# Two of a transformer layer's matrix products by Strassen's scheme, with sums of weights made in DRAM

## The chip, the cores and the metric

The kernel runs on one core of one Trainium2 chip. A core has engines that each work through a queue of their own: TensorE (PE, matrix products into PSUM), VectorE (DVE) and ScalarE (ACT, elementwise work), GpSimd (POOL, elementwise work and some DMAs), and SyncE (SP, here the queue that issues most DMAs). They meet by semaphores: an instruction that has to wait holds up all that stand behind it on its engine. The metric is device time in microseconds for one execution, and lower is better.

## The reference

One layer with sliding-window attention over 512 positions, width 2048, and a gated per-layer embedding. All is float32.

```python
hn = rmsnorm(x, norm_g)
q, k, v, gate = split(hn @ w_in)                     # 2048, 256, 256, 2048 columns
# 32 heads of 64 in 4 groups, blocks of 128 positions, window 128:
scores = q @ k.T * 64 ** -0.5 + rel_bias[bucket]     # own block and the one before
probs  = softmax of scores with one sink per head    # causal, inside the window
y = (probs @ v * silu(gate)) @ w_out                 # 512 x 2048 by 2048 x 2048
x = x + y
emb = p @ ple_proj                                   # 512 x 256 by 256 x 2048
g = sigmoid(rmsnorm(x, ple_norm) @ ple_gate)         # 512 x 2048 by 2048 x 2048
x = x + emb * g
out = rmsnorm(x, final_g)
```

The change is in the two products with w_out and ple_gate, and in how the loads are ordered.

## The kernel before

Matrix products keep float32 accuracy in three passes: an operand is split into hi (rounded to the fast format `fp32r`) and lo (the rest), and `mm3` (L113 to 117) issues hi x hi, lo x hi and hi x lo. So each product of 128 x 128 by 128 x 512 is three matmuls.

The weights come in pieces of 128 x 1024 float32 (512 KB). The class `Weights` makes each: SP loads it into `wraw` (L85), ACT casts it to `whi` (L86), DVE subtracts to get `wlo` (L87). Each of the three names has three buffers, and pieces are made two ahead of their use.

The stages follow one another on PE:

1. The start (L160 to 205): 16 steps over the 128-row blocks of x transposed, which make the first columns of q, all of k and v, in eight PSUM banks. Then the evacuation: q is split (`qe`, `qo`, L214 to 217), the scale per position `rb` is read out, k and v are scaled, split and stored as `K`, `V` and `DV` (L232 to 273), with small subtractions on POOL (L235).
2. The projections of the other q and gate columns (L426 on), 30 groups of 16 steps of three matmuls. They are interleaved with the 64 blocks of attention: `steps` (L456) places the scores of block i, the transposition of its probabilities and their product with v between steps of the projections. Each pair of heads needs a bias tile, which SP loads from a small table in DRAM (`load_bias`, L283). When four gate columns are there, ACT applies silu to the group (L391) and POOL multiplies the four attention outputs in (`gate_value`, L388). `split_a` (L396) splits the result for the next product.
3. y: for each of the four blocks of 512 columns, 16 steps over k, each for four row blocks (L517). A piece of w_out feeds 24 matmuls. DVE adds the result to x (L529), ACT takes the squares for the norm, and x is transposed for the next stage between the steps (`turn_x`, L497).
4. g: the same with ple_gate, with the embeddings' products between. `finish` (L552 to 565) applies the sigmoid (ACT), the product with the embedding, the addition to x (DVE), the squares, and the product with final_g (POOL, L560). The last block of columns is done by row blocks (L583 on), so that the final norm and the stores of one row block run beside the next.

The order on PE is as written in the program. On the other engines, SP among them, a scheduler sets the order in the build.

Of the kernel before, what the change touches and what calls it, by code (L numbers as in the profile page):

```python
# [1 line left out]

# [15 lines left out]
D = 2048  # L18
# [15 lines left out]
WARM = 34  # L34

# [12 lines left out]
def trunk_kernel(ctx: ExitStack, tc: tile.TileContext, a: dict):  # L48
# [4 lines left out]

    const = pool("const")
    psum = pool("psum", bufs=2, space=PSUM)

    const.tile([P, 56], F32, name="pad")
    pn = const.tile([P, KC], F32, name="pn")
    acts = pool("acts", bufs=KC)
    wpool = pool("wpool", bufs=3)  # L60

# [6 lines left out]
    class Weights:  # L68


        def __init__(self, ahead):
            self.srcs, self.ahead, self.made, self.apart = [], ahead, [], set()

        def add(self, src, shape):
            self.srcs.append((src, shape))
            return len(self.srcs) - 1

        def _make(self, i):
            src, shape = self.srcs[i]
            if i in self.apart:  # L80
                return self._make_apart(i)
            raw = wpool.tile([P, WE], F32, tag="wraw", name=f"wraw{i}")
            hi = wpool.tile([P, WE], F32R, tag="whi", name=f"whi{i}")
            lo = wpool.tile([P, WE], F32R, tag="wlo", name=f"wlo{i}")
            nc.sync.dma_start(raw if len(src.shape) == 2 else raw.rearrange("p (k c) -> p k c", k=shape), src)  # L85
            nc.scalar.copy(hi, raw)  # L86
            nc.vector.tensor_sub(lo, raw, hi.bitcast(F32))  # L87
            v = lambda t: t.rearrange("p (k c) -> p k c", k=shape)
            self.made.append((v(hi), v(lo)))

        def _make_apart(self, i):

            raw = wpool.tile([P, WE], F32, tag="wraw", name=f"wraw{i}")
            nc.sync.dma_start(raw, self.srcs[i][0])
            his, los = [], []
            for k in range(2):
                r = raw[:, k * 512 : (k + 1) * 512]
                h = acts.tile([P, S], F32R, tag="ah", name=f"wh{i}_{k}")
                l = acts.tile([P, S], F32R, tag="al", name=f"wl{i}_{k}")
                nc.scalar.copy(h, r)  # L100
                nc.vector.tensor_sub(l, r, h.bitcast(F32))
                his.append(h)
                los.append(l)
            self.made.append((his, los))
# [35 lines left out]
    rb = const.tile([P, S], F32, name="rb")  # L140
# [16 lines left out]
    mid = ExitStack()  # L157
    kvq = mid.enter_context(tc.tile_pool(name="kvq", bufs=1))
    pre = ExitStack()
    start_pool = pre.enter_context(tc.tile_pool(name="start", bufs=3))  # L160

    for k in range(KC):
        xg = start_pool.tile([P, S + 1], F32, tag="xr", name=f"xr{k}")
# [6 lines left out]
        h = acts.tile([P, S], F32R, tag="ah", name=f"xh{k}")  # L170
        l = acts.tile([P, S], F32R, tag="al", name=f"xl{k}")
# [4 lines left out]
        wh = start_pool.tile([P, 768], F32R, tag="w0h", name=f"w0h{k}")  # L176
        wl = start_pool.tile([P, 768], F32R, tag="w0l", name=f"w0l{k}")
# [15 lines left out]
        if 3 <= k < 3 + NB:  # L193
            t = k - 3
            xn = start_pool.tile([P, D], F32, tag="xn", name=f"xn{t}", bufs=2)
# [5 lines left out]
        if k == 12:  # L201
            rcol = start_pool.tile([P, NB, P], F32, name="rcol", bufs=1)
            nc.vector.tensor_copy(rcol, rstd1.unsqueeze(2).to_broadcast([P, NB, P]))
# [22 lines left out]
    def evac_v():  # L226
        heads = lambda v: v.rearrange("p (h d) -> p h d", h=KVH)
        whole = []
        for t in range(NB):
            src = heads(v_ps[t][:, :256])  # L230
            whole.append(start_pool.tile([P, KVH * HD], F32, name=f"whole{t}", bufs=1))
            nc.vector.tensor_scalar_mul(heads(whole[t]), src, rstd1[:, t : t + 1])  # L232
        for t in range(1, NB):
            diff = start_pool.tile([P, KVH * HD], F32, name=f"diff{t}", bufs=1)
            nc.gpsimd.tensor_sub(diff, whole[t], whole[t - 1])  # L235
            for dst, v in ((V[t - 1], whole[t - 1]), (DV[t], diff)):
# [4 lines left out]
    relb = start_pool.tile([HEADS, BUCKETS], F32, name="relb", bufs=1)  # L241
    nc.gpsimd.dma_start(relb, a["rel"])
    tvec = start_pool.tile([HEADS, TOEP], F32, name="tvec", bufs=1)
# [17 lines left out]
    for t in range(2):  # L261
        kt = start_pool.tile([P, S], F32, tag="kt", name=f"kt{t}", bufs=1)
# [134 lines left out]
    def split_a(c):  # L397
        src = gates[c // 4][:, c % 4, :]
        ah[c] = acts.tile([P, S], F32R, tag="ah", name=f"ah{c}")
        al[c] = acts.tile([P, S], F32R, tag="al", name=f"al{c}")  # L400
        nc.scalar.copy(ah[c], src)
        nc.vector.tensor_sub(al[c], src, ah[c].bitcast(F32))

# [10 lines left out]
    for kind, c in kinds:  # L414
        for n in range(2):
            W.add(a["w_gate_in" if kind == "g" else "w_q"][c][:, n * WE : (n + 1) * WE], 8)
    for j in range(4):
        for n in range(8):
            W.add(a["w_out"][j, n], 2)
    for j in range(4):  # L420
        proj_w = a["ple_proj"].rearrange("(k p) d -> p k d", p=P)[:, :, j * 512 : (j + 1) * 512]
        if j == 3:
            W.add(proj_w, 2)
        for n in range(8):
            W.add(a["ple_gate"][j, n], 2)
        if j < 3:  # L426
            W.add(proj_w, 2)
    W.apart = set(range(len(W.srcs) - 8, len(W.srcs) - 2))

    def projections():  # L430
        for m, (kind, c) in enumerate(kinds):
            ps = bank(f"{kind}ps{c}", "p")
            for k in range(KC):
                wh, wl = W.get(2 * m + k // 8)
                mm3(ps, wh[:, k % 8, :], wl[:, k % 8, :], xh[k], xl[k], k == 0, k == KC - 1)
                if k == KC - 1:
                    if kind == "q":
                        evac_q(c, ps)
                    else:
                        g = c // 4  # L440
                        if c % 4 == 0:
                            gates[g] = apool.tile([P, 4, S], F32, name=f"gate{g}")
# [3 lines left out]
                if m == len(kinds) - 1 and k < 12:  # L446
                    split_a(k)
# [19 lines left out]
    for i in range(blocks):  # L467
# [3 lines left out]
        steps(i, todo)  # L471
    steps(blocks, 7)
    steps(blocks + 1, 7)
# [4 lines left out]
    for c in range(12, PAIRS):  # L478
        split_a(c)
    mid.close()  # L480


    late = pool("late", reuse_waits="tile")
    nc.gpsimd.dma_start(pn, a["ple_norm"])
    fg = late.tile([P, D], F32, name="fg")
    nc.gpsimd.dma_start(fg, a["final_g"].partition_broadcast(P))
    pTh = late.tile([P, 2, S], F32R, name="pTh")
    pTl = late.tile([P, 2, S], F32R, name="pTl")

    ssq2 = const.tile([P, NB, 4], F32, name="ssq2")  # L490
    ssq3 = const.tile([P, NB, 5], F32, name="ssq3")
    x1, hh, hl = [], {}, {}
    for j in range(4):
        x1.append(late.tile([P, NB, 512], F32, name=f"x1_{j}"))
        nc.sync.dma_start(x1[j], a["x"].rearrange("(t p) d -> p t d", p=P)[:, :, j * 512 : (j + 1) * 512])

    HALVES = ("sstt", "ppoo")  # L497

    def turn_x(k):

        j, kk = divmod(k, 4)
        tp = bank(f"tp{k}", HALVES[j % 2][kk])
        for t in range(NB):
            nc.tensor.transpose(tp[:, t * P : (t + 1) * P], x1[j][:, t, kk * P : (kk + 1) * P], ident)
        pl_, th, tl = (late, f"hh{k}", f"hl{k}") if j < 3 else (acts, "ah", "al")
        hh[k] = pl_.tile([P, S], F32R, tag=th, name=f"hh{k}")
        hl[k] = pl_.tile([P, S], F32R, tag=tl, name=f"hl{k}")
        nc.scalar.mul(hh[k], tp, pn[:, k : k + 1])
        nc.vector.scalar_tensor_tensor(
            out=hl[k], in0=tp, scalar=pn[:, k : k + 1], in1=hh[k].bitcast(F32), op0=ALU.mult, op1=ALU.subtract  # L510
        )

    def blk(t):
        return slice(t * P, (t + 1) * P)

    wi = 2 * len(kinds)
    turning = []  # L517
    for j in range(4):
        acc = [bank(f"y{j}_{t}", HALVES[j % 2][t]) for t in range(NB)]
        for k in range(KC):  # L520
            wh, wl = W.get(wi + k // 2)
            for t in range(NB):
# [131 lines left out]
```

## Time and profile before

| what | value |
|---|---|
| median of 3 runs | 865.29 us (864.97 to 866.22) |
| the profiled execution | 863.4 us, span 861.7 us |
| mean granted TensorE clock | 0.998 |
| busy: PE / DVE / ACT / POOL | 849.0 / 494.1 / 368.3 / 108.4 us |
| the start | 0 to 76 us |
| projections and attention | 76 to 474 us |
| y (w_out) | 474 to about 656 us |
| g (ple_gate and embeddings) | about 656 to 853 us |
| after the last matmul | 853 to 862 us |

Times in rows of the profile are microseconds from the start of the span unless marked ns. A row of a group gives the line, the engine, the operation with its tiles (out<-in), the shapes, the count, then the busy time and the mean duration in ns, then the idle time before it and what ended it. A row of a timeline begins with its start and its duration. Matmuls are pipelined, so their durations overlap.

### The profile page before, as it was taken

How to read it: one execution, taken by the hardware profiler on the slowest of the kernel's cores; microseconds unless marked ns; L12 is line 12 of the kernel's file. 1: busy time of each engine (PE TensorE's matmuls, PEld its weight loads, DVE VectorE, ACT ScalarE, POOL GpSimd, SP SyncE). 2: the span in 40 equal slices, each digit the busy share in tenths (PEclk: the TensorE clock that was granted, in tenths of full speed). 3: DMA queues.
4: the chain of work that ended last, by engine and by line, in shares of the span. 5: the costliest groups of instructions: out<-in, count | busy, mean ns of one | idle time of the engine just before them, and what ended most of it. 6: DMA issues, size and time to landing. Idle time of an engine off the chain costs nothing.

```text
span 861.7 us, 11068 instructions
## 1 busy us (share of the span) xinstructions
PE 849.0 (99%) x4182; PEld 712.2 (83%) x4182; DVE 494.1 (57%) x835; ACT 368.3 (43%) x740; POOL 108.4 (13%) x177
## 2 busy tenths in 40 slices
PE   8999999999999999999999999999999999999995
PEld 7888888888888888888888888888888888888885
DVE  4556777777776877777878524232434252343734
ACT  5644444645436544446536424131424242324513
POOL 3001111222111311114111200000000020020311
PEclk9999999999999999999999999999999999999999
DMA  8870322322232222222222822222223223223222
GB/s 307 302 248 2 110 74 98 99 86 86 86 103 87 91 86 86 94 90 86 86 86 86 339 98 76 97 98 99 96 75 122 98 83 112 98 97 126 95 98 98
DMA packets 33509, 96.75 MB, mean 112 GB/s; under 512 B 3328, under 2 KB 7584, under 8 KB 32816
## 3 DMA queue, kind: packets, MB, share of 16 engines
q1 hardware_dynamic: 33184, 94.92, 31.7%
q0 software_dynamic: 272, 1.13, 0.4%
q8 instruction: 33, 0.54, 0.3%
q14 instruction: 20, 0.16, 0.1%
HBM read 91.79 MB, written 4.24 MB: 111 GB/s over the span
## 4 chain that ended last, share of the span: by engine, by line
PE 92%; DVE 4%; DMA 2%; ACT 1%; issue 1%; SPq 0%; DVEq 0%; ACTq 0%
PE qps L117 7%; PE y L117 7%; PE y L116 7%; PE y L115 7%; PE qps L116 7%; PE qps L115 7%; PE g L116 6%; PE g L117 6%; PE g L115 6%; PE gps L116 6%; PE gps L115 6%; PE gps L117 6%; PE o L366 3%; PE s L304 3%; PE pt L339 2%; DMA w<-in_w_first 1%
## 5 line engine op out<-in xcount | busy, mean ns | idle before, releaser
L87 DVE TENSOR_TENSOR wlo<-wraw,whi 128x1024 fp32r<-128x1024 f32 x122 | 154.1, 1264 | 189.7 <-ACT whi L86 188.7
L86 ACT CAST whi<-wraw 128x1024 fp32r<-128x1024 f32 x122 | 127.9, 1049 | 206.9 <-PE y L117 94.0
L115 PE MATMUL gps<-xh,whi 128*128 128x512 f32 x256 | 102.9, 402 | 0.0
L115 PE MATMUL y<-whi,ah 128*128 128x512 f32 x256 | 100.8, 394 | 0.0
L116 PE MATMUL gps<-xl,whi 128*128 128x512 f32 x256 | 100.3, 392 | 0.0
L117 PE MATMUL gps<-xh,wlo 128*128 128x512 f32 x256 | 100.1, 391 | 0.0
L117 PE MATMUL y<-whi,al 128*128 128x512 f32 x256 | 99.9, 390 | 0.0
L116 PE MATMUL y<-wlo,ah 128*128 128x512 f32 x256 | 99.7, 389 | 0.0
L327 ACT ACTIVATE t<-t,sm 128x129 f32<-128x129 f32 x128 | 50.6, 397 | 94.6 <-DVE sm L324 94.4
L115 PE MATMUL qps<-xh,whi 128*128 128x512 f32 x224 | 90.5, 404 | 0.0
L116 PE MATMUL qps<-xl,whi 128*128 128x512 f32 x224 | 87.8, 392 | 0.0
L117 PE MATMUL qps<-xh,wlo 128*128 128x512 f32 x224 | 87.8, 392 | 0.0
L115 PE MATMUL g<-whi,hh 128*128 128x512 f32 (+1 forms) x212 | 82.0, 387 | 0.0
L116 PE MATMUL g<-wlo,hh 128*128 128x512 f32 (+1 forms) x212 | 81.8, 386 | 0.1
L117 PE MATMUL g<-whi,hl 128*128 128x512 f32 (+1 forms) x212 | 81.7, 386 | 0.0
L560 POOL TENSOR_TENSOR x<-x,fg 128x512 f32<-128x512 f32 x12 | 19.5, 1650 | 304.9 <-ACT sg L559 304.9
L117 PEld LDWEIGHTS gps<-xh,wlo 128*128 128x128 f32 x256 | 48.1, 188 | 10.5
L117 PEld LDWEIGHTS y<-whi,al 128*128 128x128 f32 x256 | 48.0, 188 | 10.1
L116 PEld LDWEIGHTS y<-wlo,ah 128*128 128x128 f32 x256 | 48.1, 188 | 9.8
L115 PEld LDWEIGHTS y<-whi,ah 128*128 128x128 f32 x256 | 48.1, 188 | 9.7
L116 PEld LDWEIGHTS gps<-xl,whi 128*128 128x128 f32 x256 | 48.4, 189 | 6.8
L115 PEld LDWEIGHTS gps<-xh,whi 128*128 128x128 f32 x256 | 48.2, 188 | 6.9
(156 smaller groups left out, 1509.2 us busy)
## 6 DMA issues: line engine op xcount, KB each, us to landing
wraw<-in_w_gate_in SPq DMA_DIRECT2D x32, 512.0 KB, 3.6
wraw<-in_w_out SPq DMA_DIRECT2D x32, 512.0 KB, 3.2
wraw<-in_ple_gate SPq DMA_DIRECT2D x32, 512.0 KB, 3.2
wraw<-in_w_q SPq DMA_DIRECT2D x28, 512.0 KB, 3.3
w<-in_w_first SPq DMA_DIRECT2D x15, 384.0 KB, 5.6
xr<-in_xT SPq DMA_DIRECT2D x16, 256.5 KB, 5.7
xn<-in_x SPq DMA_DIRECT2D x4, 1024.0 KB, 7.5
bias<-tdram SPq DMA_DIRECT2D x16, 256.0 KB, 3.3
```

The costliest lines, as they stand in the source:

```text
L86: nc.scalar.copy(hi, raw)
L87: nc.vector.tensor_sub(lo, raw, hi.bitcast(F32))
L115: nc.tensor.matmul(ps, sh, mh, start=first, stop=False)
L116: nc.tensor.matmul(ps, sh, ml, start=False, stop=False)
L117: nc.tensor.matmul(ps, sl, mh, start=False, stop=last)
L304: nc.tensor.matmul(s_ps[:, e, :], st, K[kv][:, keys, low], start=low == 0, stop=low == 1)
L327: nc.scalar.activation(te, te, AF.Exp, bias=sm[:, e : e + 1], accum_out=sm[:, 2 + e : 3 + e])
L339: nc.tensor.transpose(pt[:, e, :], t[:, e, 1:], ident)
L366: nc.tensor.matmul(ops[:, n % 2], st, pr[:, low], start=b == low == 0, stop=low == 1 and b == len(parts) - 1)
L560: nc.gpsimd.tensor_mul(xt, xt, fg[:, j * 512 : (j + 1) * 512])
```

## The change

**Products.** Both large products go by Strassen's scheme in Winograd's form. The 512 rows, the 2048 inner positions and the 2048 columns are each cut in two, and seven products of half size take the place of eight. A `unit` is one of the seven for one half of its columns: two PSUM banks (128 rows x 512 columns each), four pieces of weights, 48 matmuls. There are 14 units to a product, in the order p = 1, 7, 2, 6, 3, 5, 4 for w_out and 1, 2, 7, 6, 3, 5, 4 for ple_gate.

**Sums of activations.** `Forms` makes the left operand of each p: where it needs a sum or difference, two subtractions on DVE of 128 x 4 x 256 in place, then four splits of 128 x 512 (ACT and DVE). They are written one step per piece of the unit before.

**Sums of weights.** Those for p = 7 and p = 5 are made in DRAM during attention: `sum_weights(i)` issues in every second block one copy from DRAM to DRAM on SP, and in the others one accumulating DMA on POOL. Those for p = 6 and p = 4 grow in SBUF: the eight pieces of p = 7 (`seed`) are loaded into tiles `grown`, and after each is used a DMA on POOL adds another block of weights to it (`grow`).

**Results.** `add_y` and the code of the gate combine the seven results: ACT copies, DVE additions out of PSUM and POOL additions in SBUF, each written one unit later. The gate's sigmoid then reads an SBUF tile.

**Memory and queues.** Large tiles of the start, the gates and the transposed x share one pool of four (`whole`). The split halves of x transposed lie in two pools of eight. The buffers of `w0l` in the start go from three to two. The order of SP's queue is now as written, as PE's is. The first bias load is written ahead of the projections' loads.

The core of the diff:

```diff
+    ctx.enter_context(tc.manual_schedule(engines={mybir.EngineType.PE, mybir.EngineType.SP}))
...
-    acts = pool("acts", bufs=KC)
+    whole = pool("whole", bufs=4)
     wpool = pool("wpool", bufs=3)
+    acts = pool("acts", bufs=KC // 2)
+    mid = ExitStack()
+    more = mid.enter_context(tc.tile_pool(name="more", bufs=KC // 2))
...
+        wl = start_pool.tile([P, 768], F32R, tag="w0l", name=f"w0l{k}", bufs=2)
...
+    def sum_weights(i):
+
+        if i % 2 == 0 and i // 2 < len(copies):
+            nc.sync.dma_start(*copies[i // 2])
+        elif i % 2 == 1 and 0 <= i // 2 - 1 < len(adds):
+            nc.gpsimd.dma_start(*adds[i // 2 - 1], accum_op=ALU.add, max_dma_last_dim=8192)
...
+        def _prepare(self, i):
+            kind, src, key = self.specs[i]
+            if kind == "grow":
+                t = self.grown[key]
+                nc.gpsimd.dma_start(t, src, accum_op=ALU.add)
+            else:
+                if kind == "seed":
+                    t = self.grown[key] = rooms[0].tile([P, WE], F32, tag="grown", name=f"grown{i}", bufs=8)
+                else:
+                    t = wpool.tile([P, WE], F32, tag="wraw", name=f"braw{i}")
+                nc.sync.dma_start(t.rearrange("p (k c) -> p k c", k=2) if kind == "proj" else t, src)
+            self.base[i] = t
...
+    class Forms:
...
+                src, sub = {
+                    1: (lo1, None), 7: (lo1, (hi1, lo1)), 2: (lo2, None), 6: (lo1, (hi2, lo1)),
+                    3: (lo2, (lo2, lo1)), 5: (hi1, (hi1, hi2)), 4: (hi2, None),
+                }[p]
+                if sub:
+                    nc.vector.tensor_sub(src, *sub)
+                    yield
+                for n in range(2):
+                    v = src[:, 2 * n : 2 * n + 2]
+                    fh = acts.tile([P, 2, 256], F32R, tag="ah", name=f"fh{self.nm}{p}_{h}{n}")
+                    fl = acts.tile([P, 2, 256], F32R, tag="al", name=f"fl{self.nm}{p}_{h}{n}")
+                    nc.scalar.copy(fh, v)
+                    nc.vector.tensor_sub(fl, v, fh.bitcast(F32))
+                    self.made[p].append((fh, fl))
+                    yield
...
         scores(i)
         steps(i, todo)
+        sum_weights(i)
...
+    def unit(p, jj, at, forms, todo):
+
+        ps = banks()
+        f = forms.made[p]
+        for m in range(4):
+            bh, bl = B.get(at[p, jj] + m)
+            for kk in range(2):
+                k = 2 * m + kk
+                fh, fl = f[m]
+                for tb in range(2):
+                    mm3(ps[tb], fh[:, kk, blk(tb)], fl[:, kk, blk(tb)], bh[kk], bl[kk], k == 0, k == 7)
+            some_later(4 - m)
+            todo()
+        return ps
...
+    def add_y(p, jj, tb, ps):
+        own = lambda j, t: x1[j][:, t, :]
+        c11, c12, c21, c22 = (own(2 * v + jj, 2 * u + tb) for u in range(2) for v in range(2))
+        u2, u3 = s1[:, jj, tb, :], s7[:, jj, tb, :]
+        if p == 1:
+            nc.scalar.copy(u2, ps)
+            nc.gpsimd.tensor_add(c11, c11, u2)
+        elif p == 7:
+            nc.scalar.copy(u3, ps)
+        elif p == 2:
+            nc.vector.tensor_add(c11, ps, c11)
+            squares(tb, jj)
+        elif p == 6:
+            nc.vector.tensor_sub(u2, ps, u2)
+            nc.gpsimd.tensor_add(u3, u3, u2)
+        elif p == 3:
+            nc.vector.tensor_add(c12, ps, c12)
+            nc.gpsimd.tensor_add(c12, c12, u2)
+            nc.gpsimd.tensor_add(c22, c22, u3)
+        elif p == 5:
+            nc.vector.tensor_add(c12, ps, c12)
+            squares(tb, 2 + jj)
+            nc.vector.tensor_add(c22, ps, c22)
+            squares(2 + tb, 2 + jj)
+            nc.gpsimd.tensor_sub(c21, c21, u3)
+        else:
+            nc.vector.tensor_add(c21, ps, c21)
+            squares(2 + tb, jj)
```

436 lines of the change are left out of this document (287 added, 149 removed).

## The prediction

> **What bounds the kernel now.** I read the page's busy times and the chain that ended last, then what TensorE (PE) waited for, then the windows by stage.
>
> ```profile
> PE 849.0 (99%) x4182; PEld 712.2 (83%) x4182; DVE 494.1 (57%) x835; ACT 368.3 (43%) x740; POOL 108.4 (13%) x177
> ...
> PE 92%; DVE 4%; DMA 2%; ACT 1%; issue 1%; SPq 0%; DVEq 0%; ACTq 0%
> ```
> ```profile
> PE qps L115 <- ACT w0h L179: 1.8, 1, 1.8
> ...
> PE pt L339 <- ACT whi L86: 0.5, 1, 0.5
> ```
> ```profile
> core 0: us, PE busy (x) PEld busy (x) DVE busy (x) ACT busy (x) POOL busy (x), PEclk, DMA share, GB/s
> ...
> 97.00:474.00 377.00, 377.00 (x1924) 317.45 (x1924) 284.11 (x549) 188.79 (x481) 65.34 (x120) 1.00 0.27 90
> ...
> 517.00:683.00 166.00, 166.00 (x763) 137.25 (x763) 58.74 (x68) 52.97 (x80) 0.00 (x0) 1.00 0.28 96
> ```
> PE is busy for 99% of the span, its waits are of 1.8 us and less, and its granted clock is 1.00: from start to end the kernel is as long as its matmuls. While it multiplies by w_out (517 to 683) VectorE (DVE) is busy 59 us of 166, ScalarE (ACT) 53, GpSimd (POOL) not at all. So matmuls left out are time won, as long as the others keep PE fed with the work they get instead. The sum below is made against the profiled run, 863.4 us (span 861.7), 1.9 us under the median of 865.29.
>
> **The matmuls that go.** One row per matmul:
>
> ```profile
> 473.97 0.40 PE L115 MATMUL y<-whi,ah 128*128 128x512 f32 x1
> ...
> 482.14 0.39 PE L115 MATMUL y<-whi,ah 128*128 128x512 f32 x1
> ```
> The durations overlap; what counts is the interval. From the first to the second of these lie 36 matmuls, 8.17/36 = 0.227 us each. Each product goes from 16 x 4 x 4 x 3 = 768 such matmuls to 7 products x 2 column halves x 48 = 672. The embeddings and transposes stay. 2 x 96 x 0.227 = **-43.6 us**. A piece of the weights (512 KB) now feeds 12 matmuls, 2.72 us of PE, where it fed 24.
>
> **The start.** Loads now go out in written order, and the first bias load is written ahead of the first three pieces of the weights. In the built order it waits for the start's last matmul, because its tile lies where the start's tiles were. The three pieces stand behind it on SP, and on DVE their splits stand behind the whole evacuation of the start. Before, they had been split long ahead:
>
> ```profile
> 55.65 1.23 DVE L87 TENSOR_TENSOR wlo<-wraw,whi 128x1024 fp32r<-128x1024 f32 x1 [2.37 <-ACT whi L86]
> 56.79 0.95 DVE L180 TENSOR_TENSOR w0l<-w,w0h 128x768 fp32r<-128x768 f32 x1
> 57.66 1.22 DVE L87 TENSOR_TENSOR wlo<-wraw,whi 128x1024 fp32r<-128x1024 f32 x1
> ```
> ```profile
> 75.35 0.60 PE L205 MATMUL vps<-ident,rcol 128*128 128x128 f32 x4
> 75.71 0.49 PE L115 MATMUL gps<-xh,whi 128*128 128x512 f32 x1
> 76.03 0.40 PE L116 MATMUL gps<-xl,whi 128*128 128x512 f32 x1
> 76.27 0.40 PE L117 MATMUL gps<-xh,wlo 128*128 128x512 f32 x1
> ```
> ```profile
> 72.64 1.39 DVE L215 TENSOR_TENSOR qe<-qps,qe 64x512 fp32r<-64x512 f32 x2 [7.92 <-ACT qe L214]
> ...
> 86.57 1.39 DVE L273 TENSOR_TENSOR K<-kt,K 64x512 fp32r<-64x512 f32 x2
> 87.99 1.23 DVE L87 TENSOR_TENSOR wlo<-wraw,whi 128x1024 fp32r<-128x1024 f32 x1
> ```
> ```profile
> wraw<-in_w_gate_in SPq DMA_DIRECT2D x32, 512.0 KB, 3.6
> ```
> ```profile
> L87 DVE TENSOR_TENSOR wlo<-wraw,whi 128x1024 fp32r<-128x1024 f32 x122 | 154.1, 1264 | 189.7 <-ACT whi L86 188.7
> L86 ACT CAST whi<-wraw 128x1024 fp32r<-128x1024 f32 x122 | 127.9, 1049 | 206.9 <-PE y L117 94.0
> ```
> The third matmul of the projections needs wlo; it began at 76.27. Now DVE works through the same evacuation from 72.64 to 87.96 (it hardly idled in it) and only then splits: 87.96 + 1.23 = 89.2, a loss of **+12.9 us**. The low end, if DVE took the split as soon as it can be had: load issued at 75.6, landed 3.6 later, cast 1.05, split 1.23, is 81.5, a loss of 5.2. The high end adds the two casts of the weights that now stand on ACT ahead of the last casts of V, 2.1 us: 15.0. I take the middle value because the order on DVE is fixed and the whole evacuation has its row. From there on PE is as it was; the pieces behind follow every 5.4 us or more, and a split costs DVE 1.2.
>
> **The end of the projections.** The last gate group goes through silu on ACT, then four multiplications on POOL. In the built order DVE has two subtractions, gate1 with gate3 (p = 6's form), ahead of the split of the fourth piece (blo3), and they wait for the last of the four.
>
> ```profile
> L443 DVE TENSOR_TENSOR gate<-gps,rb x16: 670/681/692, 89.1 to 474.2; 128x512 f32<-128x512 f32 x16
> L388 POOL TENSOR_TENSOR gate<-gate,u x16: 1280/1303/2264, 158.2 to 482.9; 128x512 f32<-128x512 f32 x16
> ...
> L391 ACT ACTIVATE gate<-gate x4: 1917/1918/1919, 156.2 to 476.7; 128x2048 f32<-128x2048 f32 x4
> ```
> The last multiplication began at 482.9 and ends at 484.2. Two subtractions of 1024 elements a row at 1.23 (L87's size) and the split at 1.23 end at 487.9. PE reads blo3 in its 38th matmul, at 473.97 + 37 x 0.227 = 482.4: **+5.5 us**. No row shows a subtraction of this shape; with half or one and a half of that duration the ends are 4.3 and 6.7. The load of one seed piece on SP waits for the same multiplication and has 24 us of lead: nothing.
>
> **DVE and ACT in the two products.** Counted in the built order, by rows of before:
>
> ```profile
> L402 DVE TENSOR_TENSOR al<-gate,ah x16: 673/684/1559, 463.9 to 485.4; 128x512 fp32r<-128x512 f32 x16
> ```
> ```profile
> L529 DVE TENSOR_TENSOR x<-y,x 128x512 f32<-128x512 f32 x16 | 10.9, 692 | 4.3 <-PE y L117 4.3
> ...
> L605 DVE TENSOR_SCALAR x<-x,y,nw 128x512 f32<-128x512 f32 x16 | 7.7, 542 | 0.2
> ```
> ```profile
> 701.60 1.22 DVE L87 TENSOR_TENSOR wlo<-wraw,whi 128x1024 fp32r<-128x1024 f32 x1
> ...
> 755.23 0.68 DVE L556 TENSOR_TENSOR sg<-e,sg 128x512 f32<-128x512 f32 x1
> 755.94 1.08 DVE L557 TENSOR_TENSOR x<-x,sg 128x512 f32<-128x512 f32 x1
> 756.94 2.31 DVE L87 TENSOR_TENSOR wlo<-wraw,whi 128x1024 fp32r<-128x1024 f32 x1
> ```
> ```profile
> 753.47 6.95 POOL L560 TENSOR_TENSOR x<-x,fg 128x512 f32<-128x512 f32 x4 [40.33 <-ACT sg L559]
> ```
> w_out: 57 splits of a piece x 1.22, 27 splits of forms x 0.68, 24 additions x 0.69, the subtractions: some 107 us of PE's 672 x 0.227 = 152.5. ple_gate: 59 x 1.22, 21 x 0.68, 8 subtractions x 1.23, some 51 operations of 512 x 0.65 to 0.69, the scaling at the end 16 x 0.54, small ones: some 145 us of 152.5 + 96 x 0.227 (embeddings) = 174. Beside POOL's multiplications the split took 2.31 in place of 1.22, so each of POOL's additions may cost DVE 1.1 us: 20 in the first product, 21 in the second, which makes 129 of 152 and 168 of 174. ACT, with 1.05 for the cast of a piece, has less to do than DVE. On the whole DVE keeps up; by the piece it doesn't always: a piece lasts 2.72 us, the splits run two pieces ahead, so a run of DVE work over some 5.4 us longer than PE's comes through. Low end 0; high end all that contention as stall where DVE is dense, 23. I take **+6**, two for the first product and four for the second, nearer to the low end since the totals fit.
>
> [...]
>
> **Weights' sums, and what hides them.** In attention SP gets 32 copies in DRAM and POOL 32 accumulating DMAs, one of each per two blocks of 5.9 us (377/64); in the products POOL issues 32 loads that add into SBUF, SP two thirds more pieces. The nearest rows:
>
> ```profile
> wraw<-in_w_out SPq DMA_DIRECT2D x32, 512.0 KB, 3.2
> ...
> x<-in_x SPq DMA_DIRECT2D x4, 1024.0 KB, 9.8
> ...
> fg<-in_final_g POOLq DMA_DIRECT2D x1, 1024.0 KB, 7.6
> tdram<-tvec POOLq DMA_DIRECT2D x1, 48.0 KB, 6.0
> ```
> ```profile
> L486 POOL DMA_DIRECT2D fg<-in_final_g x1 | 0.6, 584 | 0.0
> ```
> A copy goes out some 2.5 blocks (15 us) before POOL waits for it ahead of its mask and sink work, which has about one block to spare; on SP the next weights wait behind, three pieces ahead of use. At 3.2 to 9.8 us nothing shows; DMAs were busy 27% of that window at 90 GB/s, and copies (17 MB) and sums (34) add 133. POOL, 65 us busy of 377, issues 32 more at 0.6. I take 0. An adding load is issued when its piece is used, and needed 6 pieces (16 us) later at the nearest, in ple_gate: 0 too. The start phase has two buffers of w0l in place of three: its PE window shows no wait on them, 0. At the end one more half-width subtraction: +0.3.
>
> **Sum:** 863.4 - 43.6 + 12.9 + 5.5 + 6 + 0.3 = 844.5, against the median 1.9 more: **846.4 us**, 2.2% faster.
>
> **Rivals.** (a) The two transitions cost less: the split at the start goes as soon as it can, DVE gets to blo3 in time, the products show no stall: 863.4 - 43.6 + 5.2 + 0.3 + 1.9 = 827.2. For it: most of DVE's cover elsewhere; against it: the built order.
> (b) Slower: the adding loads become the bound. Each has its destination to read as well, 1 MB in all, for which the row of x shows 9.8 us. Done one after another at s us, the eight of ple_gate's p = 6 stall PE by 8s - 35.4 (13 pieces of 2.72), w_out's by 8s - 57.2. From s = 7.0 the 20.6 us to no change are gone; at 9.8 it is 43 + 21 = 64 more: 910 us. For it: no row shows such a DMA. Against: 3.2 us for 512 KB, and rows are latencies that overlap.
> (c) The change does less than it says on PE: excluded, the built order has 192 matmuls fewer.
>
> **How the numbers follow.** The forecast's own range takes all low ends, 831, to all high ends, 866: 0.71. Rival (a) 0.07, rival (b) 0.13; 0.04 lies near no change, 0.05 slower by other stalls. The range 829 to 870 leaves out part of (a) and most of (b). Faster by over 0.2% 0.78, within 0.2% (about what can be told: three runs lie 0.14% apart) 0.04, slower 0.18.
>
> **What would show it.** Right: PE with 192 matmuls of 512 columns fewer; one wait of PE of some 13 us at 76 for wlo, one of 5 to 6 us some 8 us after the projections end, for DVE; waits of some us in ple_gate's p = 6 to 5, for DVE's splits. Wrong: PE waiting in attention for POOL's or SP's work; waits for braw or grown behind a DMA; a run without the wait at 76.

## The result and the profile after

The changed kernel takes 860.2 us (median; 858.98 to 861.14), the kernel before 865.13: a ratio of 0.994, with a 95% interval of 0.9921 to 0.9958. That is 0.6% faster where 2.2% was forecast. The time lies in the range, at 829 to 870, and the sign is right, but seven tenths of the gain are missing; the range holds it by its width, which was meant for longer waits and not for what is found here. The profiled execution took 861.1 us, with a span of 859.2.

The page of the changed kernel, its busy times, the granted clock by fortieths of the span, and the engines' shares of the chain that ended last:

```profile
span 859.2 us, 11291 instructions
...
PE 818.4 (95%) x3972; PEld 682.9 (79%) x3972; DVE 624.4 (73%) x948; ACT 447.5 (52%) x862; POOL 204.2 (24%) x265
...
PEclk9998899999999999999999989999999999999988
...
PE 76%; DVE 11%; ACT 5%; DMA 4%; issue 2%; POOL 1%; SPq 0%; DVEq 0%; ACTq 0%; POOLq 0%
```

Two lines of the two pages give the whole account. PE was busy 849.0 of 861.7 us before and is busy 818.4 of 859.2 now. The matmuls left out are worth 43.6 us, so PE should be busy 849.0 - 43.6 = 805.4. It is busy 13.0 more than that: its matmuls take longer. And it is idle for 859.2 - 818.4 = 40.8 us where it was idle for 12.7: 28.1 more. The three make -43.6 + 13.0 + 28.1 = -2.5 us, the difference of the two spans. The clock line shows where matmuls take longer, and the chain, with 92% on PE before, now has a quarter elsewhere. The clock line before was:

```profile
PEclk9999999999999999999999999999999999999999
```

What PE waited for, in the changed kernel (sum, count, longest):

```profile
PE u L108 <- DVE blo L480: 10.0, 4, 4.9
PE gps L107 <- ACT whi L94: 7.8, 1, 7.8
PE gps L109 <- DVE wlo L95: 4.6, 1, 4.6
PE pt L331 <- DVE t L321: 3.5, 2, 3.1
PE last L108 <- DVE blo L480: 1.9, 2, 1.4
...
PE o L358 <- POOL own L339: 0.6, 2, 0.5
PE last L107 <- DVE nw L797: 0.5, 1, 0.5
```

The longer ones where they end, in PE's timeline (start, duration, what ran, in brackets the idle time before it and what ended it):

```profile
300.19 0.66 PE L331 MATMUL pt<-ident,t 128*128 128x128 f32 x2 [3.05 <-DVE t L321]
...
506.80 0.80 PE L108 MATMUL u<-blo,fho 128*128 128x512 f32 x1 [4.89 <-DVE blo L480]
...
589.88 0.57 PE L108 MATMUL u<-blo,fho 128*128 128x512 f32 x1 [2.99 <-DVE blo L480]
...
823.70 0.50 PE L108 MATMUL u<-blo,fhg 128*128 128x512 f32 x1 [1.51 <-DVE blo L480]
```

And stretches that begin where one of these waits ends (each line: from and to, length, then busy time and instruction count of PE, PEld, DVE, ACT and POOL, the granted clock, the DMAs' share and rate):

```profile
87.98:91.98 4.00, 4.00 (x10) 3.18 (x11) 2.22 (x2) 0.00 (x0) 0.00 (x0) 0.52 0.66 176
...
300.19:304.19 4.00, 4.00 (x14) 3.38 (x15) 2.79 (x6) 1.33 (x6) 2.10 (x3) 0.59 0.74 136
506.80:511.80 5.00, 5.00 (x12) 3.94 (x13) 2.21 (x2) 0.59 (x1) 0.52 (x1) 0.51 0.83 272
589.88:593.88 4.00, 4.00 (x11) 3.13 (x12) 3.83 (x5) 0.00 (x0) 0.86 (x1) 0.57 0.59 92
823.70:827.70 4.00, 4.00 (x18) 3.31 (x19) 3.90 (x9) 3.39 (x7) 1.51 (x1) 1.00 0.00 0
831.51:839.51 8.00, 7.45 (x19) 5.42 (x20) 8.00 (x11) 2.03 (x5) 3.38 (x2) 0.57 0.36 133
```

After the waits of 4.58, 3.05, 4.89 and 2.99 us the granted clock is 0.5 to 0.6 in these stretches, and PE gets through 10 or 11 matmuls of 512 columns in 4 us, where 17.6 have room. This "half clock" lasts 3 to 5 us. At the end three shorter waits follow one another (0.48, 1.36 and 0.55 us, between 829 and 834); there it begins at 832.5, ahead of the third, and lasts until 839. After the wait of 1.51 (at 823.70) the clock is 1.00. A stretch of 4 us with 10 matmuls costs 4 - 10 x 0.227 = 1.7 us; the one at 506.80 costs 2.3, that at 589.88 1.5, that at 831.51, less its 0.55 of idle time, 3.1, and that at 300.19, where short matmuls stand between, some 1.8 by the spacing of the long ones. That is 10.4 of the 13.0. The two matmuls between the first two waits, at 82.19, took 1.22 us in place of 0.45, 0.8 more.

So the mean clock fell from 0.998 to 0.977, in stretches that follow the kernel's own waits. That the idle time is the cause is shown by the run with fillers below.

### The profile page after: what moved, and what is told of

Read it like the earlier page. It is cut to its first block, busy times and chain, and to the rows that moved or that the text cites. A ratio compares the mean times of both kernels' runs of the same rounds, so it can differ in the third digit from the quotient of the medians.

```text
span 859.2 us, 11291 instructions
## 1 busy us (share of the span) xinstructions
PE 818.4 (95%) x3972; PEld 682.9 (79%) x3972; DVE 624.4 (73%) x948; ACT 447.5 (52%) x862; POOL 204.2 (24%) x265
## 3 DMA queue, kind: packets, MB, share of 16 engines
q1 hardware_dynamic: 37056, 121.13, 40.1%
## 4 chain that ended last, share of the span: by engine, by line
PE 76%; DVE 11%; ACT 5%; DMA 4%; issue 2%; POOL 1%; SPq 0%; DVEq 0%; ACTq 0%; POOLq 0%
PE u L108 11%; PE u L109 11%; PE u L107 11%; PE qps L108 5%; PE qps L107 5%; PE qps L109 5%; PE gps L109 5%; PE gps L107 5%; PE gps L108 5%; DVE blo L480 2%; PE o L358 2%; PE s L296 2%; DVE wlo L95 1%; PE pt L331 1%; ACT whi L94 1%
## 5 line engine op out<-in xcount | busy, mean ns | idle before, releaser
L480 DVE TENSOR_TENSOR blo<-braw,bhi 128x1024 fp32r<-128x1024 f32 x70 | 93.4, 1337 | 27.4 <-ACT bhi L479 27.0
L95 DVE TENSOR_TENSOR wlo<-wraw,whi 128x1024 fp32r<-128x1024 f32 x60 | 75.2, 1256 | 31.6 <-ACT whi L94 30.8
L108 PE MATMUL u<-blo,fho 128*128 128x512 f32 x224 | 89.3, 398 | 8.6 <-DVE blo L480 8.5
L479 ACT CAST bhi<-braw 128x1024 fp32r<-128x1024 f32 x70 | 73.5, 1050 | 43.2 <-PE u L109 28.6
L107 PE MATMUL u<-bhi,fho 128*128 128x512 f32 x224 | 89.1, 398 | 0.0
L109 PE MATMUL u<-bhi,flo 128*128 128x512 f32 x224 | 88.8, 397 | 0.0
L480 DVE TENSOR_TENSOR blo<-grown,bhi 128x1024 fp32r<-128x1024 f32 x46 | 69.5, 1515 | 21.7 <-ACT bhi L479 21.7
L108 PE MATMUL u<-blo,fhg 128*128 128x512 f32 x208 | 81.1, 390 | 1.5 <-DVE blo L480 1.5
L107 PE MATMUL u<-bhi,fhg 128*128 128x512 f32 x208 | 81.3, 391 | 0.0
L109 PE MATMUL u<-bhi,flg 128*128 128x512 f32 x208 | 81.0, 390 | 0.0
```

The lines of the kernel that those rows point to most:

```text
L107: nc.tensor.matmul(ps, sh, mh, start=first, stop=False)
L108: nc.tensor.matmul(ps, sh, ml, start=False, stop=False)
L109: nc.tensor.matmul(ps, sl, mh, start=False, stop=last)
```

## The experiments

Theory A: the time missing against the matmul count is the sum of separate waits, each with a cause that can be taken away by itself, and each wait of some 3 us or more carries some 2 us of half clock. The rival varies by place and stands in the expectations.

The experiments ran on several chips, and each ratio is against the kernel before on the same one, where it took 863.65 to 865.04 us; the changed kernel's ratio is 0.994. The intervals are about 0.002 to either side, so the times of two runs whose ratios lie less than some 0.003 apart (2 to 3 us) don't tell them apart by themselves. There the traces decide, at the place of the edit; each is of one execution.

**The start: the first pieces of the weights loaded early.** The specs of the projections' weights are written ahead of the start, and the first pieces are asked for at its step 12.

```diff
+    for kind, c in kinds:              # moved here from behind the start
+        for n in range(2):
+            W.add(a["w_gate_in" if kind == "g" else "w_q"][c][:, n * WE : (n + 1) * WE])
     for k in range(KC):
...
+        if k == 12:
+            W.get(0)
```

> The first three pieces of the projections' weights are loaded from the start's twelfth step on, ahead of the first bias load; nothing else is changed. Theory A (a wait of PE costs its idle time and then some 2 us of matmuls at half the clock): the two waits at 74 to 88 us (7.8 and 4.6) and the half clock until 92 go together, the projections begin at once, and the profiled time falls from 861.1 by some 13 to 14 to about 847.5. Theory B (the supply of split weights is the bound, and a wait that is taken away comes back at the next piece): less than half of that, 855 or more, with a new wait of PE for a split in the first 30 us of the projections.

847.45 us, a ratio of 0.9799 (0.9779 to 0.982). The two waits of 7.8 and 4.6 are gone, and the clock's first 8s with them. One new wait of 2.2 at 95, for the cast of a later piece, carries some 1.7 us of half clock. So some 12 us (0.994 against 0.98 of 865) hung on this one written order.

**The start: the waits filled with idle matmuls.** 120 and 70 small bf16 matmuls into a bank of their own, ahead of the first matmul of the projections and ahead of the third. They change neither what PE waits for nor when it is there.

```diff
+    fill = bank("fill", "p")
+    for _ in range(120):
+        nc.tensor.matmul(fill[:, :P], ones, ones, start=True, stop=True)
     proj = projections()
```

> 190 small bf16 matmuls on a tile of ones are put into PE's two waits at the start (120 ahead of the first matmul of the projections, 70 ahead of the third); everything that PE waits for stays as it is. Theory A (the granted clock falls because PE is idle): the third matmul of the projections begins at 88 as before, the matmuls behind it come every 0.23 us and not every 0.43, and the time falls by about 2, to 859. Theory B (those matmuls are slow for another reason, such as splits that come late one after another): the interval stays at 0.43 until 92 and the time stays at 861 or above.

858.3 us, a ratio of 0.9935 (0.9914 to 0.9957). The whole time can't tell 2 us here; the timeline of PE can. First the changed kernel, then the one with the fillers, and its window behind the wait:

```profile
82.19 0.79 PE L107 MATMUL gps<-xh,whi 128*128 128x512 f32 x1 [7.81 <-ACT whi L94]
...
87.98 0.79 PE L109 MATMUL gps<-xh,wlo 128*128 128x512 f32 x1 [4.58 <-DVE wlo L95]
88.58 0.63 PE L107 MATMUL gps<-xh,whi 128*128 128x512 f32 x1
...
91.92 0.40 PE L109 MATMUL gps<-xh,wlo 128*128 128x512 f32 x1
```
```profile
88.54 0.50 PE L579 MATMUL gps<-xh,wlo 128*128 128x512 f32 x1 [1.14 <-DVE wlo L95]
88.88 0.39 PE L107 MATMUL gps<-xh,whi 128*128 128x512 f32 x1
```
```profile
88.54:92.54 4.00, 4.00 (x18) 3.31 (x19) 2.22 (x2) 0.00 (x0) 0.00 (x0) 1.00 0.74 190
```

From 88.58 on the matmuls follow each other every 0.43 us in the changed kernel, until 91.92. With the fillers wlo comes at the same time, within 0.6 us, and they follow every 0.23 us at once: 18 in 4 us instead of 10. So the slow stretch comes from PE's idle time before it, not from the data or the DMAs beside it. The interval is nearly twice as long (0.43 against 0.23 us) at a granted clock of 0.52 against 1.00, and the clock was back 3 to 5 us after the single waits ended. In the changed kernel single waits of 2.99 and 3.05 us were enough for it, and one of 1.51 was not.

**The end of the projections: gate1 - gate3 on POOL.** The two subtractions that wait for POOL's last multiplication go behind it on POOL itself, so that DVE gets to the split of the fourth piece without them.

```diff
-                    nc.vector.tensor_sub(src, *sub)
+                    (nc.gpsimd if self.nm == "o" and h == 1 and p in (6, 5) else nc.vector).tensor_sub(src, *sub)
```

> The two subtractions that wait for the last gate (those of gate1 with gate3, for p = 6 and p = 5) go from DVE to POOL, behind the multiplications that they wait for. Theory A: PE's wait of 4.9 us at 507 and the 2.5 us of half clock behind it go, but for about 0.6 that the load of the fourth piece may leave: 7 less, 854. Theory B: DVE is slowed by POOL's longer subtractions and the wait stays at over half: 858 or more.

857.33 us, a ratio of 0.992 (0.9905 to 0.9935): between the two, and by the time alone not clear of the changed kernel. In the changed kernel, DVE's rows show the wait that the prediction named, with the splits behind it:

```profile
503.25 2.36 DVE L551 TENSOR_TENSOR gate<-gate,gate 128x1024 f32<-128x1024 f32 x2 [5.32 <-POOL gate L380]
505.52 3.49 DVE L480 TENSOR_TENSOR blo<-braw,bhi 128x1024 fp32r<-128x1024 f32 x3
```

With the subtractions on POOL, DVE's and POOL's rows are:

```profile
500.71 7.64 DVE L480 TENSOR_TENSOR blo<-braw,bhi 128x1024 fp32r<-128x1024 f32 x3 [3.08 <-ACT bhi L479]
```
```profile
504.01 6.62 POOL L551 TENSOR_TENSOR gate<-gate,gate 128x1024 f32<-128x1024 f32 x2
```

DVE no longer waits for POOL, only for ACT's cast. But the same three splits, which now run beside POOL's multiplications and subtractions, take 7.64 us where they took 3.49. PE's one wait of 4.9 becomes three of 1.2, 0.3 and 2.4. The cause is the right one, and POOL is no free place for the work.

**The end of the projections: DVE's order kept as written.** The same subtractions stay on DVE but may not be moved ahead of the splits.

```diff
-                    nc.vector.tensor_sub(src, *sub)
+                    ins = nc.vector.tensor_sub(src, *sub)
+                    if self.nm == "o" and p in (6, 5):
+                        tc.keep_in_program_order(ins)
```

> The subtractions for p = 6 and p = 5 of w_out stay on DVE and are held in written order, so that none stands ahead of the splits of the first pieces; nothing else. Theory A (DVE's wait for the last gate behind which the fourth split stands is the cause of PE's 4.9 at 507): the wait falls to 1.5 or less, what POOL's gate multiplications take from the split beside them, no half clock follows, 6 less, about 854. Theory B (the pieces land too late there anyway, or POOL holds up the splits as in the run with the subtractions on POOL): over 3 us in waits and half clock remain in the first 30 us of the product, 857 or above.

860.34 us, a ratio of 0.9958 (0.9944 to 0.9972): theory A's time missed, theory B's range met. The wait of 4.9 shrinks to 1.1, as theory A has it, but another takes its place 14 us on: PE waits 3.2 us for the cast of w_out's eighth raw piece. ACT's row shows that it waits for that piece's load:

```profile
515.40 1.04 ACT L479 CAST bhi<-braw 128x1024 fp32r<-128x1024 f32 x1 [4.39 <-DMA braw<-in_w_out]
```

Behind the 4.9 us that wait had been hidden. What holds the load is tested further on.

**w_out: twelve additions of p = 6 and 3 from POOL to DVE.**

```diff
-            nc.gpsimd.tensor_add(u3, u3, u2)
+            nc.vector.tensor_add(u3, u3, u2)
...
-            nc.gpsimd.tensor_add(c12, c12, u2)
-            nc.gpsimd.tensor_add(c22, c22, u3)
+            nc.vector.tensor_add(c12, c12, u2)
+            nc.vector.tensor_add(c22, c22, u3)
```

> In the w_out product the twelve additions in SBUF for p = 6 and p = 3 go from POOL to DVE; nothing else. Theory A (two splits that took 4.5 and 5.5 us, where 1.2 is usual, were held up by POOL's additions on a shared access to SBUF): all splits there take 1.2, PE's wait of 3.0 at 587 and the half clock behind it go, 5 less, about 855, though DVE has 8 us more to do. Theory B (those splits were long because the adding DMA wrote or the piece was late): the long splits stay, and with DVE's added work the wait grows: 861 or above.

856.09 us, a ratio of 0.9911 (0.9889 to 0.9932). Giving the fuller engine more work made the kernel no slower, and some 3 us faster by the ratios, just about what they can tell; PE's wait of 2.99 is gone. Before the wait of 2.99 at 589.88, DVE's and POOL's rows of the changed kernel are:

```profile
579.26 4.54 DVE L480 TENSOR_TENSOR blo<-grown,bhi 128x1024 fp32r<-128x1024 f32 x1 [0.30 <-ACT bhi L479]
...
584.33 5.50 DVE L480 TENSOR_TENSOR blo<-grown,bhi 128x1024 fp32r<-128x1024 f32 x1
```
```profile
578.62 2.85 POOL L706 TENSOR_TENSOR s7o<-s7o,s1o 128x512 f32<-128x512 f32 x2
581.12 1.59 POOL L710 TENSOR_TENSOR x<-x,s7o 128x512 f32<-128x512 f32 x1
...
584.68 1.61 POOL L710 TENSOR_TENSOR x<-x,s7o 128x512 f32<-128x512 f32 x1
585.93 2.80 POOL L716 TENSOR_TENSOR x<-x,s7o 128x512 f32<-128x512 f32 x2
```

And DVE's with the additions on DVE itself:

```profile
580.05 0.68 DVE L706 TENSOR_TENSOR s7o<-s7o,s1o 128x512 f32<-128x512 f32 x1
580.65 1.22 DVE L480 TENSOR_TENSOR blo<-grown,bhi 128x1024 fp32r<-128x1024 f32 x1
```

A split that takes 1.22 us alone lasts 4.54 and 5.50 beside three POOL additions in a row. Each ends 1.1 us after POOL's last addition does (582.71 and 588.73), about its own length. The second split lost 4.3 us (5.50 less 1.22) while POOL's three additions ran for 4.05 (584.68 to 588.73): as if it stood still for all of them. The first lost 3.3 us of the 3.45 that POOL still had to go when its row began. An addition costs POOL some 1.4 to 1.6 us and holds DVE for about as long; on DVE itself four of them took 0.68, 1.79, 1.78 and 0.68 us between 580 and 588. In all, DVE is busy 618.6 us with the twelve additions and 624.4 without them. Who comes first can't be read here: the second split's row begins 0.35 us before POOL's first addition and still ends last. Nor do the rows show what the two engines share; "a shared access to SBUF" in theory A was the author's guess.

**ple_gate: the product with final_g into DVE's last scaling.** The 16 multiplications by final_g on POOL go; DVE's scaling by the row's factor and a constant (two scalars) becomes one by the row's factor and final_g's row.

```diff
-        nc.gpsimd.tensor_mul(xt, xt, fg[:, j * 512 + c.start : j * 512 + c.stop])
...
+        nc.vector.tensor_mul(y, y, nw)
...
-        nc.vector.tensor_scalar(xt, xt, y, nw, op0=ALU.mult, op1=ALU.mult)
+        nc.vector.scalar_tensor_tensor(
+            out=xt, in0=xt, scalar=y, in1=fg[:, j * 512 : (j + 1) * 512], op0=ALU.mult, op1=ALU.mult
+        )
```

> The changed kernel, with the multiplication by final_g taken from POOL and folded into DVE's last scaling (one instruction with a scalar and a tensor in place of one with two scalars, 128x512 as before; one more multiplication of 128x1). In the changed kernel PE lost 7.8 us in the last 30 us of ple_gate: waits of 1.5, 0.5, 1.4 and 0.6 for DVE's splits at 823 to 834, and matmuls at half the clock behind them. Theory A: DVE falls behind there because its instructions take longer beside POOL's multiplications (the splits of 128x1024 take 1.5 between 800 and 840, against 1.22 elsewhere). Without them the waits shrink to about 1 in all, no half clock follows, and the time is about 854 (852 to 857). Theory B: DVE has too much of its own work there, whatever POOL does. Then the waits stay, and the time is 859 to 861.

855.74 us, a ratio of 0.9915 (0.9898 to 0.9931). The same 20 us windows, first of the changed kernel, then without POOL's multiplications (this run is some 3 us ahead by then):

```profile
800.00:820.00 20.00, 20.00 (x90) 16.43 (x89) 20.00 (x25) 13.40 (x22) 8.58 (x5) 1.00 0.16 52
820.00:840.00 20.00, 16.10 (x55) 11.75 (x54) 19.89 (x31) 10.88 (x18) 6.40 (x4) 0.83 0.18 67
```
```profile
800.00:820.00 20.00, 20.00 (x90) 16.57 (x89) 17.78 (x28) 14.65 (x26) 0.00 (x0) 1.00 0.13 43
820.00:840.00 20.00, 18.91 (x107) 16.14 (x106) 17.78 (x40) 11.08 (x19) 0.00 (x0) 1.00 0.30 106
```

DVE was busy without a gap and did 56 instructions; now it does 68 in less time, PE's longest wait there is 1.0 us, and the clock stays at 1.00. At POOL's share of 43% in the first window DVE had looked full by its own work; it was full of POOL's: the splits of 128x1024 took 1.49 to 1.54 us on average between 800 and 840 beside POOL's multiplications, and take 1.22 without them.

**Attention: no sums in DRAM.** The copies and accumulating DMAs are left out, and p = 7 and 5 load single blocks of the weights instead of sums, so the output is not the layer's.

```diff
-                    t = summed[nm, p, jj, m] = tc.dram_tile([P, WE], F32, name=f"{nm}_{p}_{jj}_{m}")
-                    copies.append((t, block(nm, *parts[0], jj, m)))
-                    adds.append((t, block(nm, *parts[1], jj, m)))
```

> Leaves out the sums of weights that are made in DRAM: no copies and no accumulating DMAs in attention, and p = 7 and p = 5 read one block of the weights in place of the sum. Theory A (their traffic makes the projections' weights land late, 6.1 and 7.1 us in place of 3.6 and 3.3, and that causes PE's waits in attention): landing goes back below 4 us, the waits at 203, 300 and 421 with the half clock behind the longest go, 6 less, about 855. Theory B (SP's written order is the cause: weights stand behind bias loads that wait for DVE): landing falls, the wait at 300 stays at 2 us or more, 859 to 861.

857.21 us, a ratio of 0.9918 (0.9903 to 0.9933). It gains 2 to 3 us, less than theory A has it: of the two waits for t the one at 300 remains, at 2.4 us, as theory B has it, though no half clock follows it (the clock is 1.00 there).

**Attention: the bias load written later.** It is written behind the third block of a pair of heads, not the first.

```diff
-        if n == 0 and c + 1 < PAIRS:
+        if n == 2 and c + 1 < PAIRS:
             load_bias(c + 1)
```

> The bias load of the next pair of heads is written at the third block of a pair in place of the first; nothing else. Theory A (SP stands up to 22 us at these loads until DVE has freed the tile, then issues five DMAs in a burst, so a piece of weights lands late, its cast holds up ACT, and the exponentials behind it): no wait of SP of over some us at this line, landing of the projections' weights below 5 us, PE's wait at 300 and the half clock behind it gone: 5 less, about 856. Theory B (the wait at 300 comes from silu and its tables, 4.5 us of ACT ahead of the exponentials, and from POOL's gate multiplications beside DVE, whatever the loads do): 2 to 3 us of wait remain, 859 to 861.

855.79 us, a ratio of 0.9899 (0.9883 to 0.9916). SP's waits for its bias load, the landing time of the gate weights, and ACT's cast ahead of PE's wait at 300, in the changed kernel; then the first two here (the last number of a landing is the median from issue to landing):

```profile
SPq L281 <- DVE sc L305: 241.0, 14, 22.0
...
wraw<-in_w_gate_in SPq DMA_DIRECT2D x32, 512.0 KB, 6.1
...
291.10 1.05 ACT L94 CAST whi<-wraw 128x1024 fp32r<-128x1024 f32 x1 [3.20 <-DMA wraw<-in_w_gate_in]
```
```profile
SPq L281 <- DVE sc L305: 68.1, 14, 7.7
...
wraw<-in_w_gate_in SPq DMA_DIRECT2D x32, 512.0 KB, 4.5
```

In the changed kernel the bias load stands on SP until the last scores of the old bias tile are read, up to 22 us, and the weights and copies behind it then go out together: six transfers from 284.44 to 287.40. The cast at 291 waited for one of them, and the chain through silu, DVE's t and PE's wait at 300 follows from it. With the load written later that cast waits for no DMA and the wait at 300 is 0.6. The order in which the loads left mattered at least as much as the sums' traffic: the run without the sums moves 33.6 MB less, but SP's waits for the bias load stay at 239 us and the weights land in 4.5 (gate) and 6.0 us (q), where the order alone brings 4.5 and 4.6.

**All of them.** Early first pieces, late bias load, DVE's order kept, the additions on DVE, final_g in DVE's scaling.

> Together: the first pieces loaded early, the bias loads written later, the subtractions in written order, the twelve additions on DVE, and the product with final_g taken from POOL into DVE's last scaling (17 POOL multiplications fewer, 16 scalings that read one operand more). If the losses are separate they add up: 13 for the start, 3 to 6 in attention, 6 at the end of the projections, 5 at 587, 3 to 5 in the last 30 us: 829 (from 826 to 833). If they share a cause (DVE is short of time as a whole), less than half of what comes behind the start, 840 or more.

833.91 us, a ratio of 0.9645 (0.9627 to 0.9663). It is just above the expected range: PE waits 3.2 us for w_out's eighth raw piece here too.

**And the seed pieces and final_g loaded later.** The adding pieces' first halves (p = 7's seeds, but for the first) are written behind that raw piece's load, and the load of final_g, 1 MB, waits for a block of x that w_out's product p = 2 finishes.

```diff
-... kind != "grow" and (kind == "seed" or n <= i + 3):
+... kind != "grow" and (kind == "seed" and (n == 8 or i >= 4) or n <= i + 3):
...
+            nc.gpsimd.tensor_copy(fg[:1, :1], x1[0][:1, 0, :1])
             nc.gpsimd.dma_start(fg, a["final_g"].partition_broadcast(P))
```

> The kernel e9_all with two loads moved out of the end of the projections: the seed pieces of p=7, but for the first, are written behind the load of the eighth raw piece of w_out, and the load of final_g (1 MB on POOL's queue) is made to wait for a block of x that w_out's second product finishes. In e9_all the eighth raw piece's load landed late, and PE waited 3.2 us for its split at 498, with some 3 us of half clock behind. Theory A: that load was late because 1 MB of x, 1 MB of final_g and the seed pieces were in flight with it. With two of these gone, the wait shrinks to under 1, no half clock follows, and the time is about 828 (826 to 830). Theory B: it is late by its own start (SP gets to it late, or its buffer is free late). Then the wait stays and the time is 833 to 835.

827.32 us, a ratio of 0.9582 (0.9567 to 0.9597): 4.2% faster than the kernel before, and faster than the changed kernel by 3.6%. From its page, and what PE still waits for:

```profile
PE 806.9 (98%) x3972; PEld 676.3 (82%) x3972; DVE 613.7 (74%) x964; ACT 448.0 (54%) x862; POOL 151.8 (18%) x237
```
```profile
PE pt L345 <- ACT whi L94: 2.2, 1, 2.2
...
PE u L108 <- DVE blo L483: 1.1, 1, 1.1
PE last L108 <- DVE blo L483: 1.0, 1, 1.0
```

The wait for the eighth raw piece is gone. That piece's load and its cast, first in the run before this one, then here:

```profile
486.10 0.33 SPq L464 DMA_DIRECT2D braw<-in_w_out  x1
...
497.01 1.04 ACT L482 CAST bhi<-braw 128x1024 fp32r<-128x1024 f32 x1 [4.41 <-DMA braw<-in_w_out]
```
```profile
487.38 0.33 SPq L464 DMA_DIRECT2D braw<-in_w_out  x1
...
494.00 1.05 ACT L482 CAST bhi<-braw 128x1024 fp32r<-128x1024 f32 x1 [2.15 <-DMA braw<-in_w_out]
```

The load leaves at the same point in both (this run is 1.3 us behind there), but the cast that waits for it starts 10.9 us later in the first and 6.6 here. So it had been late by the transfers in flight with it, not by its own start. Six seed pieces go out right behind it in both; what no longer stands ahead of it is one seed piece (at 485.02) and final_g (at 484.94). Which of the two did it is open; they were moved together. PE is busy 806.9, within 1.5 us of 805.4, and the one wait over 2 us is left with that much half clock behind it.

The account by each profile's own span and PE busy time; the slow part is the busy time less 805.4, the idle part the span less the busy time (the kernel with fillers is left out, since its fillers count as busy):

| kernel | span | slow | idle |
|---|---|---|---|
| before | 861.7 | 0 | 12.7 |
| changed | 859.2 | 13.0 | 40.8 |
| early first pieces | 846.1 | 9.5 | 31.2 |
| subtractions on POOL | 855.3 | 9.8 | 40.1 |
| DVE's order kept | 857.6 | 10.3 | 41.9 |
| additions on DVE | 854.5 | 7.9 | 41.2 |
| final_g on DVE | 853.1 | 8.2 | 39.5 |
| no sums | 855.8 | 11.2 | 39.2 |
| bias load later | 853.1 | 9.0 | 38.7 |
| all | 830.5 | 3.2 | 21.9 |
| all, seeds and final_g later | 825.3 | 1.5 | 18.4 |

Four of the single edits (the subtractions, the additions, final_g, the bias load) change the idle time by some 2 us or less and the slow time by 3 to 5. But each row is one execution, and not all of that is the edit's doing. With the additions on DVE, and with DVE's order kept, the 3.1 us of half clock at the end are missing (the clock is 1.00 there), though these edits lie in w_out and the waits at the end are as long. With the subtractions on POOL the wait of 3.0 at 588 has no half clock behind it, and with final_g on DVE the one of 2.98 in attention has none (the clock is 1.00 behind both). What is an edit's own is the wait that it takes away, and the half clock that stood behind that.

## Why the prediction was wrong

Against the profiled execution, term by term:

| term | predicted | measured |
|---|---|---|
| matmuls | -43.6 | -43.6: the interval is again 0.23 us, and PE's busy time in the last run fits it to 1.5 us |
| start | +12.9 | +11.7, the third matmul of the projections at 87.98 where it was at 76.27; and 1.7 of half clock |
| end of the projections | +5.5 | a wait of 4.9; and 2.3 of half clock |
| DVE in the products | +6 | waits of 3.7 in w_out and 3.9 in ple_gate; and 1.5 + 3.1 of half clock |
| weights' sums, attention | 0 | waits of 4.1; and 1.8 of half clock |
| tail | +0.3 | +1.1, from the last matmul's start to the end of the span |

These measured terms make -3.8 us, the two profiled executions (861.1 and 863.4) -2.3; 1.5 us stays unassigned.

- **The step that failed is a term that the sum put at nothing without a reason: the half clock behind the waits.** The sum put each wait down at its own length and the matmuls at 0.227 us throughout. The bounds of all terms were bounds of waits. Yet the forecast had a wait of 13 us and one of 5 in it, and in the trace of before no wait was longer than 1.8 us, so that trace couldn't show what a longer one does. The sum gave 844.5 us for the profiled execution, which took 861.1, 16.6 more: 10.4 of that is the half clock in the five stretches shown (13.0 by PE's busy time), 4.1 the waits in attention, 1.5 stays unassigned, and the errors of the other terms nearly cancel (-1.2 - 0.6 + 1.6 + 0.8). The half clock was told apart from the wait at the start by the fillers, which took the half clock away and left the wait's end where it was; at the other places it is read from the clock and the spacing of the matmuls.
- **"At 3.2 to 9.8 us nothing shows"** failed as well: attention was put at 0 and cost 5.9 us. The bounds took the DMAs one by one and POOL's queue; the cause was SP's queue, where the bias load, held by a reader, let weights and copies out in one burst. That the loads now go in written order was read for the start and not for the 14 bias loads behind it.
- **The start** came out as predicted, by the built order: DVE's split behind the evacuation, though as two waits, 7.8 for whi and 4.6 for wlo. The run with early pieces wins it back but for one wait of 2.2.
- **The end of the projections** came out as predicted, with the wait of "5 to 6 us" at 4.9. But its cover was thinner than "24 us of lead: nothing" says of the loads there: once the wait was gone, a late load took its place.
- **DVE in the products** at +6 against 7.6 of waits: the choice near the low end was right in size. The price of 1.1 us for a POOL addition that meets a split was too low: two splits lost 3.3 and 4.3 us, about as long as the additions beside them ran (3.45 and 4.05 us, some 1.4 each). So +6 came close with too low a price, which is in part luck.
- **Rivals.** (b), the adding loads as the bound, didn't happen: they land in 7.0 and 7.5 us, past its point of 7.0, but they overlap (three of ple_gate's were issued 2.7 us apart, at 732.36, 735.08 and 737.80), and no wait of PE goes back to them. (a), 827.2 us without the transitions' losses, is not this kernel; but the last experiment, which takes most of those losses and the others away, measures 827.3 (on a chip where the kernel before took 863.65).

## What to carry to other kernels

When a change adds a wait to an engine that was never idle, price the wait and what comes behind it: here each wait of some 3 us cost 1.5 to 2.3 us of half clock on top in most executions, and three small waits in a row could cost 3.1. Before moving work to an idle engine, ask whether that engine's instructions hold up the busy one: work for POOL cost DVE more than doing it itself (DVE was busy 624.4 us with w_out's twelve additions on POOL, 618.6 with them on DVE). Where loads go out in written order, look for the one that has to wait for a reader, and count what stands behind it.

## What the runs showed of the hardware

- The half clock began after waits of about 3 us, though not by a sharp bound. Over the traces of the changed kernel and the ten experiments it followed all 26 waits of PE of 3.05 us or more, and 13 of 17 between 2.1 and 3.0: it followed one of 2.2 us (at 95, with the early pieces) and one of 2.99, and did not follow one of 2.4 in the run without sums, nor one of 3.0 at 588 with the subtractions on POOL. The same short waits at the end were followed by it in six traces and not in two.
- A 512 KB copy from DRAM to DRAM took 6.8 us and an adding DMA into DRAM 7.1 to 7.9, into SBUF 7.0 to 7.5 (medians from issue to landing), where plain loads of that size in the same kernel took 3.2 to 8.7. All shared the DMAs with other transfers, so this doesn't show what each would take alone.
- Beside three 128x512 additions in a row on POOL, 128x1024 subtractions on DVE took 4.54 and 5.50 us in place of 1.22.
